# Odd mixer: all sixteen modulation steps behind the second direction's grams in TensorE's order

## The chip, the cores and the metric

The kernel runs on one core of one Trainium2 chip. The metric is the device time of one execution in microseconds (us); the time given for a kernel is the median of its runs. PE is TensorE (matmul), PEld its weight load, DVE VectorE, ACT ScalarE, POOL GpSimd, SP SyncE, whose queue issues nearly all DMAs of this kernel.

## What is computed

Two transformer blocks follow each other on 256 tokens and 256 context tokens of width 1024. The second block has two layers; the change lies in the last one, whose mixer ("odd") joins an RWKV-7 recurrence in both directions and a neighbourhood attention:

```python
mod = jnp.einsum('bd,de->be', jax.nn.silu(c), ada_w[i]) + ada_b[i]
sh1, sc1, g1, sh2, sc2, g2 = jnp.split(mod[:, None, :], 6, -1)
h = rms_norm_2(x, norm1_g[i]) * (1.0 + sc1) + sh1
y, yc = odd_mixer(h, hc, ...)
x = x + g1 * y
h = rms_norm_2(x, norm2_g[i]) * (1.0 + sc2) + sh2
x = x + g2 * expert_choice_ffn(h, moe_router[i], moe_w1[i], moe_w3[i], moe_w2[i])

def wkv7_step(S, inp):                      # one token, one head; the scan runs forward and in reverse
    r, w, k, v, a, b = inp
    sa = jnp.einsum('bhvk,bhk->bhv', S, a)
    S = S * w[:, :, None, :] + sa[..., None] * b[:, :, None, :] + v[..., None] * k[:, :, None, :]
    return S, jnp.einsum('bhvk,bhk->bhv', S, r)
```

The modulation `mod` depends on `c` and on the weights alone. Its last parts (`g1`, `sh2`, `sc2`, `g2`) are first needed where the mixer's result is gated and where the experts are routed, so the kernel is free to compute them at any time before.

## The kernel before

The recurrence is computed in chunks of 64 tokens. For each direction `d` (0, then 1) and each block `b` of two heads (four blocks), `rwkv` runs three parts. `decays(d, b)` multiplies the log decays with a triangular matrix on PE (`py<-tri`), takes exponentials on ACT and forms the products `AR`, `Bh`, `Kh` on DVE and POOL. `within(d, b)` makes the grams `pg<-AR,Bh` on PE and masks them on DVE into `Lx` and `Lc` (L1940). `spill(d, b)` makes the grams `pg<-AR,Kh`, masks them into `MN` (L1953), multiplies them with `V` (`py<-V,MN`), transposes `Bh` and `Kh`, and stores the results to DRAM (`sp`). Between the directions `begin(1)` runs `low_rank` (`py<-low,lwa`, `py<-lwa,low`).

`gather(d)` writes `Lx` and `Lc` to DRAM (L1995) and reads them back in another layout (L1998). `substitute(d)` then inverts 32x32 triangles in 31 steps of two operations on DVE (L2012, L2014), on `fsx` for direction 0 and `sgs` for direction 1, copies the result (L2015) and writes it to DRAM (L2016, L2017). `complete(d)` reads it back (L2031) and runs products on PE (`pg<-fsx,Lx` is its first). Then follow the chunk recurrence and, between its steps, the attention (`natten`: `pS<-nk,nq`, `pt<-cst,p`, `pd<-low,nv`), and after the mixer the sixteen experts, whose weights stream in (L1580).

The modulation is a generator of steps (`mods_steps`, L503). Inside `rwkv` one step loads four tiles `mw` of 128x512 (256 KB each, L550, on SP's queue) and multiplies each with `sil` into another 32 rows of one bank `pd` (`pd<-mw,sil`). Eight steps fill a bank; then come a copy on ACT (`modrow`), four transposes into `pS`, three small operations on DVE, one more transpose (`gatec`) and a small DMA. Two banks are left when `rwkv` begins, so it holds 16 steps: 64 tiles, 64 matmuls (128 records, since a float32 matmul leaves two). The tiles turn in five buffers (tag `n2`, which the attention's `nbias` shares). `fill(n)` takes up to n steps and does nothing when none is left.

Instructions are put in order by a scheduler: each engine's queue is filled by priority, and by readiness as the scheduler's own model has it. The priority is the place in the program, plus `OLATE` = 2000 for what `fill` issues. At run time each engine and SP's queue take their instructions strictly in that order. In the program, `fill` stands behind every block of direction 0 and of direction 1 (`OF` = (2, 2, 2)), so all 16 steps are taken by the end of `within(1, 3)`, and their instructions may go wherever the scheduler finds room.

Of the kernel before, what the change touches and what calls it, by code (L numbers as in the profile page):

```python
# [248 lines left out]
class Kernel:  # L249
# [75 lines left out]

    def mm(self, out, lhsT, rhs, start, stop):
        ins = self.nc.tensor.matmul(out, lhsT, rhs, start=start, stop=stop, skip_group_check=True)  # L327
        if self.pin:
            self.tc.keep_in_program_order(ins)
        return ins  # L330
# [1291 lines left out]

T2 = 16
SUB0, SUB1 = 0, 0
OLATE, OF = 2000, (2, 2, 2)
DECAY = math.exp(-0.5)


# [18 lines left out]
class Odd(Moe):  # L1647
# [201 lines left out]
    def rwkv(self, od, core, m):  # L1849
        nc, tc, a = self.nc, self.tc, self.a  # L1850
# [15 lines left out]
        def begin(d):  # L1866
            S = st[d]

            S["AR"] = core.tile([128, 4, 768], F32, name=f"AR{d}")
            S["ARx"] = S["AR"][:, :, :512].rearrange("p b (i k t) -> p b i k t", k=4, t=64)  # L1870
            S["sp"] = self.dram.tile([4, 128, 3, 512], F32, name=f"sp{d}")
            S["WC"] = core.tile([128, 4, 8], F32, name=f"WC{d}")
            S["gr"] = core.tile([128, 2, 4, 2, 128], F32, name=f"Lx{d}")
            S["sgs"], S["av"] = self.rates[0] if d == 0 else self.low_rank(1, core, "t2", T2, "py")
# [60 lines left out]
        def within(d, b):  # L1935

            for th in range(2):
                p, mask = gram(st[d][b][0], d, b, th)
                L = st[d]["Lc"][:, :, b] if th else st[d]["gr"][:, :, b]
                nc.vector.tensor_tensor(L.rearrange("p t h c -> p h t c"), p, mask, OP.mult)  # L1940
# [44 lines left out]
        def gather(d):  # L1985

            Lx, Lc = st[d]["gr"], st[d]["Lc"]
            scr = [self.dram.tile([4, 32, 32, 32], F32, name=f"scr{d}{i}") for i in range(3)]
            for q in range(4):
                hf, b2 = q // 2, q % 2  # L1990
                ps_ = slice(64 * hf + 32 * b2, 64 * hf + 32 * b2 + 32)
                cs = slice(32 * b2, 32 * b2 + 32)
                for i, gr in ((0, Lx[..., 64 * hf:64 * hf + 64]), (1, Lc)):
                    src = gr[ps_].rearrange("p t b h c -> p (t b h) c")[:, :, cs]
                    nc.sync.dma_start(scr[0][q, 16 * i:16 * i + 16].rearrange("u s t -> s u t"), src)  # L1995
            LM = od.tile([128, 2, 32, 32], F32, name="sgs", bufs=1) if d else st[0]["LX"]
            LM, X = LM[:, 0], LM[:, 1]
            nc.sync.dma_start(LM, scr[0].rearrange("q u s t -> (q u) s t"))  # L1998
            st[d].update(scr=scr, LM=LM, X=X)
# [51 lines left out]
        def fill(n):  # L2051
            with self.later(OLATE, "pS"):
                self.fill(n)
# [3 lines left out]
        for b in range(4):  # L2057
            if b < 3:
                decays(0, b + 1)
            if b == 2:  # L2060
                begin(1)
            within(0, b)
            spill(0, b)
            fill(OF[0])
        gather(0)
        with self.later(SUB0, "pS"):
            substitute(0)
        for b in range(4):
            decays(1, b)
            within(1, b)  # L2070
            fill(OF[1])
        gather(1)
        with self.later(SUB1, "pS"):
            substitute(1)
        for b in range(4):
            spill(1, b)
            fill(OF[2])
        with self.later(OLATE, "pS"):
            self.need(m, 2)

        td = [p.tile([128, 4, 4, 2, 64], F32, name=n, bufs=1) for p, n in ((od, "kk"), (od, "k"))]
# [187 lines left out]
```

## Time and profile before

| | |
|---|---|
| runs | 2823.29, 2827.72, 2834.02 us |
| median | 2827.72 us |
| profiled execution | 2849.02 us, of it span 2847.2 us |
| busy share of the span | PE 91%, DVE 42%, ACT 27%, POOL 11% |
| HBM read | 667.73 MB |

The profiled execution took 0.75% longer than the median; its rows are compared with its own time. The odd mixer's stretch from the first decays to the last chunk is 2041 to 2332 us of the span; the experts' weights fill the rest. In the rows, times are us from the span's start unless marked ns, and a bracket behind a row gives the engine's idle time before it and what ended it. "PEclk" is the granted clock of TensorE, 1.00 for 2.4 GHz and 0.50 for 1.2 GHz.

### The profile page before, as it was taken

What the parts mean: (1) busy time and instruction counts of PE and PEld (TensorE: products, weight loads), DVE (VectorE), ACT (ScalarE), POOL (GpSimd) and SP (SyncE); (2) the same over time, 40 slices, a digit from 0 to 9 for tenths busy, and PEclk for the clock granted to TensorE, in tenths of its full rate; (3) what the DMA queues carried; (4) which work ended last, traced back from release to release, by engine and by line L of the source; (5) the groups of instructions that cost most, each with busy time, mean ns of one, the idle gap of its engine ahead of it and who ended that gap; (6) DMA issues with size and microseconds to landing.
All of it is one profiled execution on the core that took longest, in us unless ns stands there. A gap on an engine that the chain in (4) does not pass through costs nothing.

```text
span 2847.2 us, 34601 instructions
## 1 busy us (share of the span) xinstructions
PE 2597.2 (91%) x13867; PEld 1583.0 (56%) x13867; DVE 1185.8 (42%) x2273; ACT 772.3 (27%) x1394; POOL 302.5 (11%) x370
## 2 busy tenths in 40 slices
PE   7999999997998998989799999989896997888887
PEld 4666788885766896757443333358634784212121
DVE  3355633446456567897411111164539352000000
ACT  3242322222343343376310000044432432000000
POOL 0001400004002004300100000000113130000000
PEclk8999999997999999999899999999986798999999
DMA  7443522223467754244599999942265548999998
GB/s 303 148 163 135 206 104 89 104 89 135 155 210 271 282 182 153 69 152 163 215 420 421 421 421 421 421 164 88 93 194 121 138 154 353 410 421 421 421 422 350
DMA packets 147216, 683.42 MB, mean 240 GB/s; under 512 B 38384, under 2 KB 51568, under 8 KB 71920
## 3 DMA queue, kind: packets, MB, share of 16 engines
q1 hardware_dynamic: 140656, 663.91, 60.9%
q10 hardware_dynamic: 6400, 17.31, 2.0%
q8 instruction: 109, 1.79, 0.3%
q14 instruction: 51, 0.42, 0.0%
HBM read 667.73 MB, written 11.60 MB: 239 GB/s over the span
## 4 chain that ended last, share of the span: by engine, by line
PE 55%; DMA 24%; DVE 7%; issue 2%; ACT 2%; POOL 0%; SPq 0%; ACTq 0%; DVEq 0%; POOLq 0%
DMA w<-in_moe_w 21%; PE pd L327 19%; PE pS L327 12%; PE pu L327 6%; PE pt L327 5%; PE ps L327 3%; PE pg L327 3%; PE pm L327 2%; PE ps L472 1%; DMA w<-in_ada_w 1%; DVE al L364 1%; PE pt L472 1%; DVE fs L2012 1%; PE py L327 1%; DMA w<-in_od_w_in 1%
## 5 line engine op out<-in xcount | busy, mean ns | idle before, releaser
L327 PE MATMUL pu<-w,xs 128*64 128x512 f32 (+1 forms) x2040 | 491.7, 599 | 41.3 <-DMA w<-in_moe_w 41.3
L350 DVE TENSOR_TENSOR wl<-w,wh 128x1024 fp32r<-128x1024 f32 x229 | 283.1, 1239 | 348.6 <-ACT wh L347 348.1
L347 ACT CAST wh<-w 128x1024 fp32r<-128x1024 f32 x250 | 259.5, 1041 | 603.0 <-PE pd L327 260.1
L327 PEld LDWEIGHTS pu<-w,xs 128*64 128x64 f32 (+1 forms) x2040 | 149.7, 123 | 368.8 <-issue 257.4
L327 PE MATMUL pd<-w,hidT 128*64 128x512 f32 (+1 forms) x1024 | 255.4, 598 | 30.5 <-DMA w<-in_moe_w 30.3
L327 PE MATMUL pd<-ah,wh 128*128 128x512 f32 (+2 forms) x656 | 233.6, 361 | 7.8 <-ACT wh L347 3.5
L327 PE MATMUL pd<-al,wh 128*128 128x512 f32 (+2 forms) x656 | 232.1, 355 | 8.7 <-DVE al L364 8.7
L327 PE MATMUL pd<-ah,wl 128*128 128x512 f32 (+1 forms) x648 | 227.5, 352 | 0.0
L1599 ACT ACTIVATE hid<-pu 128x512 f32<-128x512 f32 x24 | 14.2, 597 | 699.4 <-PE pu L327 699.4
L1600 DVE TENSOR_TENSOR hid<-hid,pu 128x512 f32<-128x512 f32 x24 | 16.5, 688 | 425.1 <-PE pu L327 425.1
L327 PEld LDWEIGHTS pd<-w,hidT 128*64 128x64 f32 (+1 forms) x1024 | 74.9, 122 | 201.4 <-issue 117.4
L327 PEld LDWEIGHTS pd<-ah,wh 128*128 128x128 f32 (+1 forms) x656 | 127.8, 196 | 42.8 <-issue 15.8
L327 PEld LDWEIGHTS pd<-al,wh 128*128 128x128 f32 (+1 forms) x656 | 129.0, 197 | 30.2 <-DVE al L364 10.7
L327 PE MATMUL pm<-w,sil 128*32 128x512 f32 x640 | 105.8, 700 | 40.9 <-DMA w<-in_w_mod 24.9
L327 PEld LDWEIGHTS pd<-ah,wl 128*128 128x128 f32 x648 | 127.0, 196 | 22.6 <-issue 8.2
L1609 DVE TENSOR_TENSOR ys<-pd,g 128x512 f32<-128x512 f32 x24 | 16.6, 692 | 288.7 <-PE pd L327 288.7
L1619 DVE TENSOR_TENSOR X<-X,ps 128x512 f32<-128x512 f32 x80 | 54.8, 687 | 113.3 <-PE ps L327 113.3
L1149 DVE SCALAR_TENSOR_TENSOR co<-cv,cols,co 128x512 f32<-128x512 f32 x120 | 100.6, 862 | 0.4
L327 PE MATMUL pS<-al,wh 128*128 128x256 f32 (+1 forms) x264 | 90.7, 345 | 3.7 <-DVE al L364 3.7
L327 PE MATMUL pS<-ah,wh 128*128 128x256 f32 (+1 forms) x264 | 90.0, 342 | 1.4 <-ACT ah L363 1.4
L327 PE MATMUL pS<-ah,wl 128*128 128x256 f32 (+1 forms) x264 | 89.9, 341 | 0.0
L327 PE MATMUL ps<-ys,gt 128*128 128x512 f32 x160 | 82.7, 627 | 2.1 <-DVE X L1619 2.1
(593 smaller groups left out, 4471.7 us busy)
## 6 DMA issues: line engine op xcount, KB each, us to landing
w<-in_moe_w SPq DMA_DIRECT2D x383, 1024.0 KB, 19.8
w<-in_w_mod SPq DMA_DIRECT2D x48, 1024.0 KB, 5.0
w<-in_w_up SPq DMA_DIRECT2D x32, 1024.0 KB, 5.0
w<-in_w_down SPq DMA_DIRECT2D x32, 1024.0 KB, 4.9
w<-in_ada_w SPq DMA_DIRECT2D x32, 1024.0 KB, 5.0
w<-in_w_in SPq DMA_DIRECT2D x20, 1024.0 KB, 4.9
mw<-in_ada_w SPq DMA_DIRECT2D x64, 256.0 KB, 3.7
w<-in_od_w_in SPq DMA_DIRECT2D x13, 1024.0 KB, 4.9
```

What stands on the lines that cost most here:

```text
L327: ins = self.nc.tensor.matmul(out, lhsT, rhs, start=start, stop=stop, skip_group_check=True)
L347: nc.scalar.copy(h, src)
L350: (le or nc.vector).tensor_tensor(l, src, h.bitcast(F32), OP.subtract)
L364: nc.vector.tensor_tensor(l, t, h.bitcast(F32), OP.subtract)
L472: ins = self.nc.tensor.transpose(out, in_, self.ident[:rows, :rows])
L1149: nc.vector.scalar_tensor_tensor(y, CV[:, f, :, t:t + T], self.col(f"dw{t}", f), y, OP.mult, OP.add)
L1599: nc.scalar.activation(hid[:, cs], up["moe_w1_2"][c], AF.Silu)
L1600: nc.vector.tensor_tensor(hid[:, cs], hid[:, cs], up["moe_w3_2"][c], OP.mult)
L1609: nc.vector.tensor_tensor(ys[:, cs], down[c], gate[:, cs], OP.mult)
L1619: nc.vector.tensor_tensor(self.X[tb][:, cs], self.X[tb][:, cs], ps, OP.add)
L2012: nc.vector.tensor_tensor(t, LM[:, s, tr, None].to_broadcast([128, nt_, nj]), X[:, s, None, jr].to_broadcast([128, nt_, nj]), OP.mult)
```

## The change

`fill` no longer stands among the blocks of direction 0 and behind `within(1, b)`. The sixteen steps are taken in the loop over `spill(1, b)`, four behind each block, and every PE instruction of them carries an ordering edge to the last matmul of `within(1, 3)` (`held`), so none may stand ahead of it on PE. The loads of the tiles carry no such edge: they are held by the five buffers and by their place in SP's order.

```diff
     def mm(self, out, lhsT, rhs, start, stop):
         ins = self.nc.tensor.matmul(out, lhsT, rhs, start=start, stop=stop, skip_group_check=True)
+        self.pe = ins
...
-OLATE, OF = 2000, (2, 2, 2)
+OLATE = 2000
...
             within(0, b)
             spill(0, b)
-            fill(OF[0])
         gather(0)
         with self.later(SUB0, "pS"):
             substitute(0)
         for b in range(4):
             decays(1, b)
             within(1, b)
-            fill(OF[1])
+        held = self.pe
         gather(1)
         with self.later(SUB1, "pS"):
             substitute(1)
         for b in range(4):
             spill(1, b)
-            fill(OF[2])
-        with self.later(OLATE, "pS"):
+            with tc.issue_after(held.ins):
+                fill(4)
+        with self.later(OLATE, "pS"), tc.issue_after(held.ins):
             self.need(m, 2)
```

In the changed kernel line numbers behind 327 are one higher. A row of the order is a run of equal instructions of one engine; `32x512` is one tile's matmul.

PE in direction 0, before, from the last transpose of block 0 to the first gram of block 2:

```order
L472 MATMUL py<-cst,Kh 128x128 x4
L327 MATMUL pg<-AR_13923,Kh 64x128 x2
L327 MATMUL pd<-mw,sil 32x512 x2
L327 MATMUL py<-tri,sgs 128x256
L327 MATMUL py<-tri,mix 128x256
L327 MATMUL py<-tri,sgs 128x256
L327 MATMUL py<-tri,mix 128x256
L327 MATMUL pd<-mw,sil 32x512
L327 MATMUL pg<-AR_13923,Kh 64x64 x8
L327 MATMUL pd<-mw,sil 32x512
```

The same place now:

```order
L473 MATMUL py<-cst,Kh 128x128 x4
L327 MATMUL pg<-AR_13923,Kh 64x128 x3
L327 MATMUL py<-tri,sgs 128x256
L327 MATMUL py<-tri,mix 128x256
L327 MATMUL py<-tri,sgs 128x256
L327 MATMUL py<-tri,mix 128x256
L327 MATMUL pg<-AR_13923,Kh 64x128 x2
L327 MATMUL pg<-AR_13923,Kh 64x64 x8
```

The blocks of direction 0 and 1 follow each other without `pd<-mw,sil`; all 64 of these stand further back.

PE ahead of `complete(0)`, before, from the last product of `spill(1, 3)`:

```order
L327 MATMUL py<-V,MN 64x64 x24
L472 MATMUL py<-cst,Bh 128x128 x4
L472 MATMUL py<-cst,Kh 128x128 x4
L327 MATMUL pg<-fsx,Lx_13926 64x32 x32
```

The same place now:

```order
L327 MATMUL py<-V,MN 64x64 x8
L473 MATMUL py<-cst,Bh 128x128 x4
L327 MATMUL pd<-mw,sil 32x512 x3
L473 MATMUL py<-cst,Kh 128x128 x4
L327 MATMUL pd<-mw,sil 32x512 x8
L473 MATMUL pS<-cst,modrow 128x128 x4
L327 MATMUL pd<-mw,sil 32x512 x3
L473 MATMUL pS<-cst,gatec 16x128
L327 MATMUL pd<-mw,sil 32x512 x29
L473 MATMUL pS<-cst,modrow 128x128 x4
L473 MATMUL pS<-cst,gatec 16x128
L327 MATMUL pg<-fsx,Lx_13926 64x32 x32
```

Of the 64 matmuls, 21 stand ahead of these rows, between the parts of `spill(1, b)`; the other 43 and both banks' transposes stand in them, ahead of the first product of `complete(0)`.

SP's queue where the result of `substitute(1)` goes out and comes back, before:

```order
L2016 DMA scr_15024<-sgs 128x1024
L2017 DMA scr_15025<-sgs 128x1024
L2031 DMA k<-scr_15025 32x32x32 x4
L2031 DMA sgs<-scr_15024 32x32x32 x4
L1835 DMA nbias<-in_na_bias 128x512 x3
L2134 DMA mv<-sp_13924 128x512
```

The same place now:

```order
L551 DMA mw<-in_ada_w 128x512 x2
L2017 DMA scr_14798<-sgs 128x1024
L2018 DMA scr_14799<-sgs 128x1024
L1984 DMA sp_14242<-zt 64x4x128 x4
L551 DMA mw<-in_ada_w 128x512 x3
L2032 DMA k<-scr_14799 32x32x32 x4
L2032 DMA sgs<-scr_14798 32x32x32 x4
L551 DMA mw<-in_ada_w 128x512 x33
L1836 DMA nbias<-in_na_bias 128x512 x4
L2135 DMA mv<-sp_13924 128x512
```

Of the 64 loads, 28 stand ahead of `substitute(1)`'s result (5 ahead of the first block, 6 behind the gather of direction 1, 17 between the two substitutions' results), 3 between its way out and its way back, and 33 behind both; before, all 64 stood ahead of direction 1's gather.

## Rows read from the trace of the kernel before

**Rows 1.** Busy us by engine in stretches of the odd mixer.

```profile
core 0: us, PE busy (x) PEld busy (x) DVE busy (x) ACT busy (x) POOL busy (x), PEclk, DMA share, GB/s
2041.00:2084.00 43.00, 37.83 (x398) 17.54 (x398) 19.46 (x32) 16.38 (x48) 16.05 (x17) 0.94 0.73 219
2084.00:2107.00 23.00, 23.00 (x40) 5.21 (x43) 7.31 (x14) 8.18 (x13) 0.00 (x0) 0.50 0.32 95
2119.00:2176.00 57.00, 41.05 (x417) 22.10 (x417) 47.95 (x108) 19.60 (x54) 24.78 (x23) 0.76 0.53 145
2176.00:2204.00 28.00, 16.96 (x258) 14.53 (x256) 26.21 (x73) 5.76 (x12) 3.85 (x3) 0.62 0.65 147
2202.00:2246.00 44.00, 44.00 (x559) 31.57 (x559) 16.83 (x39) 15.68 (x31) 1.80 (x1) 0.50 0.51 127
2246.00:2332.00 86.00, 86.00 (x974) 72.01 (x973) 44.00 (x92) 36.24 (x72) 25.36 (x34) 0.99 0.44 131
```

**Rows 2.** Chain that ended last, 2041 to 2119 us, shares by line.

```profile
by line: PE pd L327 36.5%; PE py L327 28.7%; DMA mw<-in_ada_w 19.4%; PE pg L327 8.8%; DMA fsx<-scr 8.3%; PE py L472 3.0%; PE pS L472 1.7%; ACT tri L1863 0.7%; SPq L550 0.4%; issue 0.4%; SPq L1998 0.1%
```

**Rows 3.** PE in order of time, direction 0 and low_rank: start, us.

```profile
2062.54 0.39 PE L327 MATMUL py<-tri,sgs 128*128 128x256 f32 x1
...
2070.60 0.67 PE L327 MATMUL pg<-AR,Bh 64*64 64x128 f32 x16
...
2072.78 0.66 PE L472 MATMUL py<-cst,Bh 128*128 128x128 f32 x4
...
2084.36 3.78 PE L327 MATMUL py<-low,lwa 64*128 64x512 f32 x4
...
2089.91 2.07 PE L327 MATMUL py<-low,lwa 64*128 64x512 f32 x2
...
2108.71 1.12 PE L327 MATMUL py<-lwa,low 64*128 64x512 f32 x2
```

**Rows 4.** DVE in order of time: grams masked, substitutions' first and last steps.

```profile
2049.51 0.68 DVE L1940 TENSOR_TENSOR Lx<-pg,cst 128x512 f32<-128x512 f32 x1
...
2113.30 0.42 DVE L1940 TENSOR_TENSOR Lc<-pg,cst 128x256 f32<-128x256 f32 x1 [4.74 <-PE pg L327]
...
2124.90 0.19 DVE L2012 TENSOR_TENSOR fs<-fsx 128x31 f32<-128x31 f32 x1 [7.27 <-DMA fsx<-scr]
...
2203.85 0.19 DVE L2014 TENSOR_TENSOR sgs<-sgs,fs 128x31 f32<-128x31 f32 x1
```

**Rows 5.** From issue to landing, the gathers' two read-backs (L1998).

```profile
DMA to landing us min/median/max: 3.4/5.0/6.5
```

**Rows 6.** SP's queue in order of time, with us that the run took.

```profile
2065.22 7.38 SPq L550 DMA_DIRECT2D mw<-in_ada_w  x8
...
2131.91 10.67 SPq L550 DMA_DIRECT2D mw<-in_ada_w  x9
...
2211.81 4.24 SPq L2031 DMA_DIRECT2D sgs<-scr  x4
...
2332.06 29.42 SPq L1580 DMA_DIRECT2D w<-in_moe_w  x15
```

**Rows 7.** From issue to landing, the 64 tiles mw.

```profile
DMA to landing us min/median/max: 2.6/3.7/5.9
```

**Rows 8.** PE in order of time, modulations' ends and complete's first product.

```profile
2088.07 1.91 PE L327 MATMUL pd<-mw,sil 128*32 128x512 f32 x2
...
2201.99 3.63 PE L327 MATMUL pg<-fsx,Lx 64*64 64x32 f32 x64
```

**Rows 9.** ACT behind a full bank of the modulation: start, us.

```profile
2090.02 0.59 ACT L523 COPY modrow<-pd 128x512 f32<-128x512 f32 x1 [0.83 <-PE pd L327]
```

**Rows 10.** Chain pieces of PE with the same shape at either clock: start, us, what.

```profile
2205.62 3.71 PE pS L327 x4
...
2251.75 1.91 PE pS L327 x4
```

**Rows 11.** PE at the span's beginning, where it runs modulations alone: busy, PEclk.

```profile
24.00:32.00 8.00, 4.40 (x20) 0.50 1.01 419
```

## The prediction

> **What bounds the kernel now.** I read the busy times by stretch first [rows 1], then the chain of waits, then single engines in order of time. From 2041 to 2107 us PE is busy 60.8 of 66 us, and DVE 26.8; from 2119 to 2204 it is the other way round, DVE 74.2 of 85 and PE 58.0. So the first part of the mixer waits for PE, the two substitutions wait for DVE, and from 2202 to 2332 PE is busy without a gap (44 of 44, 86 of 86) [rows 1]. The chain of the first part shows what PE does there: of 78 us 36.5% are modulation matmuls, 19.4% loads of their tiles and 0.4% their issue, together 43.9 us [rows 2]. The experts' first loads go out when the mixer ends, at 2332.06 [rows 6], so a shift of the mixer's end is a shift of the kernel's end.
>
> **What is taken away: the modulations among direction 0.** At most the whole 43.9 us goes. But the chain then shows the next-late work, and I walk through it in three pieces, each at 2.4 and at 1.2 GHz, since which clock PE is granted with this work alone no row shows.
>
> First piece, to the third block's first triangular product at 2062.54 [rows 3]. The first gram is masked at 2049.51, straight behind other DVE work, without a wait [rows 4]: nothing is won up to there. What is left on PE then are nine groups of grams, products with V and transposes, of which a gram takes 0.67 us and a block's transposes 0.66 at 2.4 GHz [rows 3]: I estimate 5.5 us for the nine, and 10 at 1.2 GHz. So the product comes at 2055.5 to 2060: 2.5 to 7 us won.
>
> Second piece, from there to `low_rank` at 2084.36 [rows 3], 21.8 us before. One block's nine groups pass, 5.5 us as before, with some 3 in which PE waits for ACT's exponentials and DVE's products, and then the last block's decays, 1.7: I estimate 10 us at 2.4 GHz and 14 at 1.2, where PE's own time covers the wait: 8 to 12 won.
>
> Third piece, `low_rank` to the last gram masked at 2113.30 [rows 3, 4], 28.9 us before. Eight products of 2.07 us at 1.2 GHz are 16.6 us, of 1.12 at 2.4 GHz 9.0 [rows 3]; there the chain through DVE and ACT is longer, some 14. With 1 us for the gram: 11 to 14 won. In sum 22 to 33 us; I take 28.
>
> The gather's read-back landed after 6.5 us among the tiles' loads and after 3.4 without [rows 5]. It has none beside it now; I take 2 us won, with 0 and 3 as ends.
>
> **What stays: the substitutions.** From 2124.90 to 2203.85 DVE inverts both triangles, 79 us [rows 4], nearly always busy [rows 1]. The modulations weigh little there: six small operations. The order of DVE puts two `MN` more of direction 0 inside (shapes that take 0.68 and 0.42 us as `Lx` and `Lc` [rows 4]), and the first decays of direction 1 are ready later against the substitution's start. I charge 3 us, with 1 and 5 as ends. `substitute(1)` so ends 28 + 2 - 3 = 27 us earlier, at 2177 instead of 2204.
>
> **What is added: the modulations behind.** Here the order of SP decides. Of 64 loads 31 can be out when `substitute(1)`'s result has been written; the other 33 stand behind its read-back, and PE has all of them ahead of `complete(0)`'s first product. Queued behind that on PE are all of the completion, the attention and the recurrence; none of it can pass. Counted from the last step of `substitute(1)`:
>
> - the read-back's last issue ends at 2211.81 + 4.24 = 2216.05, 12.2 us behind 2203.85 [rows 4, 6]: 12 us. The waits in it (copy, write, memset, read) stay;
> - five tiles go out at once, 2 us; the other 28 follow as buffers come free. Free of other work the ring made eight tiles in 7.38 us and nine in 10.67, 0.92 to 1.19 us each [rows 6]. At 1.2 GHz a group takes 1.91 us [rows 8], at 2.4 half of it, which the ring of five carries; I take 1.15, near the slower row, so 32.2 us;
> - the last lands after 3.7 us [rows 7] and is multiplied in 1.9 [rows 8];
> - the second bank's end: the copy takes 0.59 us [rows 9], then come four transposes (0.66 for such a group [rows 3], 1.1 at 1.2 GHz), three small operations on DVE and the last transpose, each behind the one before: I estimate 3.4 us.
>
> That is 12 + 2 + 32.2 + 3.7 + 1.9 + 3.4 = 55.2 us. Before, `complete(0)` began at 2201.99 [rows 8], 1.9 us ahead of that last step, since it needs direction 0 alone. So the move costs 57 us on the path and gives back 27: **30 us later**. Its ends: a ring at 0.92, PE at 2.4 GHz and a gain of 35 leave 12 + 2 + 25.8 + 3.7 + 1 + 3 + 1.9 - 35 = 14; a ring at 1.19 and a gain of 17 (22 + 0 - 5) give 58.2 - 17 = 41.
>
> Behind it nothing hides the delay: PE has no gap until 2332 [rows 1]. The attention's `nbias`, now behind the 33 loads too, lands while `complete(0)`'s first product runs (3.63 us [rows 8]); without that cover it would cost the 3.7 us of a landing [rows 7].
>
> **TensorE's clock.** From 2202 to 2246 PE is granted 0.50 all the time [rows 1], so that the same work could take less: four products of the attention take 3.71 us there and 1.91 at 2.4 GHz [rows 10]. By these shapes I estimate 17 us between the two clocks. I leave the 17 us out of the sum: modulations alone, 4.40 us busy of 8, were granted 0.50 at the span's beginning [rows 11], and between 2084 and 2107, with `low_rank` and no gap at all, 0.50 too [rows 1].
> The Trainium skill, page "TensorE: Matmul & The Clock Gate", section "Part 1: The HAM clock gate", says the opposite of such a stream: the throttled state is the default, and sustained activity releases it. By that rule the 33 tiles would bring the clock up ahead of `complete(0)`; by the rows of these two stretches they would not. By rule the sum would be smaller by those 17 us and by the faster ring; it is the first rival.
>
> **The rivals.**
> *The clock comes up and stays up* (not slower). With no modulation between them the decays run at 2.4 GHz, so that 33 + 3 - 1 = 35 us are won; the ring runs at 0.92 and PE at its fast groups, 49.4 us; and completion and attention win 17. That is 49.4 - 35 - 17 = -3, or 2846 in the profile and 2825 as a median. For it: PE was granted 0.94 on average from 2041 to 2084 [rows 1]. Against it: rows 11, the 23 us from 2084, and that the modulations were half of what kept PE busy there. It decides at `complete(0)`: if PE is granted 1.00 there, most of the loss is gone.
> *PE holds DVE up* (slower still). `spill(1, b)`'s grams now stand behind tiles whose loads SP may issue only behind `substitute(0)`'s result. If two of DVE's `MN` wait for such a tile in the middle of `substitute(1)`, each wait is a landing and a group, 3.7 + 1.9 us [rows 7, 8], and `substitute(1)` ends 11 us later: +41, 2869 as a median. For it: DVE keeps its order, and the grams of blocks 2 and 3 stand behind the 13th and the 14th tile. Against it: DVE has ten to fifteen steps to do before it asks for them.
> *The ring fills its gaps better than I think*, so that most of the 33 are in by the read-back: the order of SP forbids it.
>
> **How the numbers follow.** The sum is made against the profiled execution: 2849.0 + 30 = 2879. That execution took 0.75% longer than the median of 2827.7, and I carry the difference over: 2827.7 + 30 = 2858. A measurement of this kernel can tell about 0.5% from no change, 14 us: faster is below 2814, slower above 2842. Forecast 65%, nearly all of it slower; PE holding DVE up 12%, all slower; the clock 23%, of which about 16 within 14 us and 7 faster, since its ends reach 12 us below its value. Together faster 7%, same 17%, slower 76%. The range takes the forecast's ends of +14 and +41 and goes down into the clock's case, to +4 and up to +45: 2832 to 2873; it leaves out most of the clock's case and a part of the second rival, some 2 in 10.
>
> **What would show it.** In the profile after: the last gram of direction 0 masked between 2080 and 2091; the read-back of `gather(0)` landing in 3.4 to 5 us; the last step of `substitute(1)` near 2177 (2171 to 2187); then DVE and ACT idle while SP issues 33 tiles at 0.9 to 1.2 us each; `pg<-fsx,Lx` near 2232; and the experts' first load near 2362. Before those 33, PE idle for some microseconds, waiting for tiles. It would be wrong if `complete(0)` began before 2216, if PE were granted 1.00 there, or if the substitutions no longer took about 79 us.

## The result and the profile after

The changed kernel took 2866.41 us as a median (2859.64 to 2876.03), the kernel before 2830.68 in the same series: a ratio of 1.0133 with an interval of 1.0107 to 1.0159, so 30 to 45 us slower. A second series gave 1.0137 (1.0096 to 1.0179). The forecast was 2858 with a range of 2832 to 2873.

The profiled execution of the changed kernel took 2862.35 us, only 13 us more than that of before (2849.02). That the profiles stand 13 us apart and the medians 36 is the question of this study, and most of the answer is the clock.

The stretches of the mixer first, as in [rows 1] (the first number behind the stretch is its length, then busy us of PE, PEld, DVE, ACT and POOL, PEclk, DMA share, GB/s):

```profile
2042.00:2069.00 27.00, 19.84 (x309) 16.27 (x309) 16.69 (x28) 13.05 (x39) 12.76 (x14) 0.71 0.16 38
2069.00:2083.00 14.00, 11.72 (x47) 4.53 (x48) 9.32 (x15) 9.53 (x20) 3.78 (x5) 0.71 0.23 62
2097.00:2181.00 84.00, 51.56 (x607) 31.83 (x608) 74.89 (x176) 22.54 (x61) 27.01 (x24) 0.71 0.55 144
2181.00:2205.00 24.00, 12.47 (x30) 2.55 (x28) 0.78 (x1) 1.17 (x2) 1.80 (x1) 0.70 1.03 248
2205.00:2232.00 27.00, 22.95 (x59) 3.63 (x57) 0.45 (x3) 0.25 (x1) 0.00 (x0) 0.95 0.76 251
2238.54:2347.41 108.87, 108.81 (x1531) 89.32 (x1531) 58.44 (x121) 50.93 (x104) 25.63 (x34) 1.00 0.41 127
```

The row from 2205 to 2232 is new: DVE, ACT and POOL do nothing (0.45, 0.25 and 0 us of 27), and the kernel waits for tiles of the modulation. DVE in order of time, the rows that answer to [rows 4]:

```profile
2088.44 0.42 DVE L1941 TENSOR_TENSOR Lc<-pg,cst 128x256 f32<-128x256 f32 x1 [3.65 <-PE pg L327]
2097.17 0.19 DVE L2013 TENSOR_TENSOR fs<-fsx 128x31 f32<-128x31 f32 x1 [7.98 <-DMA fsx<-scr]
...
2180.49 0.19 DVE L2015 TENSOR_TENSOR sgs<-sgs,fs 128x31 f32<-128x31 f32 x1
```

SP's queue from the end of the second substitution, against [rows 6]: result out, three tiles, the read-back, then 33 tiles in one row of 33.98 us; the attention's `nbias` and the experts follow.

```profile
2182.88 0.42 SPq L2017 DMA_DIRECT2D scr<-sgs  x1
2183.35 0.42 SPq L2018 DMA_DIRECT2D scr<-sgs  x1
2183.87 4.23 SPq L1984 DMA_DIRECT2D sp<-zt  x4
2188.20 1.52 SPq L551 DMA_DIRECT2D mw<-in_ada_w  x3
2189.78 4.01 SPq L2032 DMA_DIRECT2D k<-scr  x4
2193.89 3.64 SPq L2032 DMA_DIRECT2D sgs<-scr  x4
2197.63 33.98 SPq L551 DMA_DIRECT2D mw<-in_ada_w  x33
2232.03 23.75 SPq L1836 DMA_DIRECT2D nbias<-in_na_bias  x4
...
2347.41 28.67 SPq L1581 DMA_DIRECT2D w<-in_moe_w  x15
```

PE at the same place, the rows that answer to [rows 8]:

```profile
2234.66 1.68 PE L327 MATMUL pd<-mw,sil 128*32 128x512 f32 x4 [0.76 <-DMA mw<-in_ada_w]
2237.02 0.66 PE L473 MATMUL pS<-cst,modrow 128*128 128x128 f32 x4 [0.68 <-ACT modrow L524]
2238.34 0.27 PE L473 MATMUL pS<-cst,gatec 128*16 128x128 f32 x1 [0.67 <-DVE gatec L537]
2238.54 2.06 PE L327 MATMUL pg<-fsx,Lx 64*64 64x32 f32 x64
```

`complete(0)` begins at 2238.54, 58.05 us behind the last step of `substitute(1)`; before, it was 1.86 us ahead of that step [rows 4, 8]. PE's waits in the tail ended with a tile, 16.8 us in eleven waits from 2181 to 2238; only at the ends of the two banks did it wait for ACT's copy (twice 0.7 us) and DVE's `gatec` (0.67).

### The profile page after: what moved, and what is told of

Read it like the earlier page. It is cut to its first block, busy times and chain, and to the rows that moved or that the text cites. A ratio compares the mean times of both kernels' runs of the same rounds, so it can differ in the third digit from the quotient of the medians.

```text
span 2860.5 us, 34616 instructions
## 1 busy us (share of the span) xinstructions
PE 2581.0 (90%) x13867; PEld 1573.6 (55%) x13867; DVE 1186.8 (41%) x2273; ACT 770.7 (27%) x1394; POOL 302.7 (11%) x370
## 4 chain that ended last, share of the span: by engine, by line
PE 55%; DMA 23%; DVE 7%; issue 2%; ACT 2%; SPq 1%; POOL 0%; ACTq 0%; DVEq 0%; POOLq 0%
DMA w<-in_moe_w 19%; PE pd L327 19%; PE pS L327 12%; PE pu L327 8%; PE pt L327 5%; PE ps L327 3%; PE pg L327 2%; PE pm L327 2%; DMA mw<-in_ada_w 1%; DVE al L365 1%; DMA w<-in_ada_w 1%; PE ps L473 1%; PE pt L473 1%; PE pO L327 1%; DVE co L1150 1%
## 5 line engine op out<-in xcount | busy, mean ns | idle before, releaser
L1620 DVE TENSOR_TENSOR X<-X,ps 128x512 f32<-128x512 f32 x80 | 54.8, 687 | 113.3 <-PE ps L327 113.3
```

The costliest lines, as they stand in the source:

```text
L1620: nc.vector.tensor_tensor(self.X[tb][:, cs], self.X[tb][:, cs], ps, OP.add)
```

## The experiments

Eleven runs were made, four of them of the two kernels without an edit, in three groups. A group shares its runs of the kernel before, so times of different groups are best compared by their ratio to it. Positions in the mixer are counted from the first `py<-tri` of direction 0, since what lies ahead of it varies by some us from execution to execution.

**The kernel before and the changed kernel, again.** No edit. Two theories on the 13 against 36 us.

> The kernel before, once more, to see a second profiled execution of the same program. In the two profiles the change cost 13 us (2849.0 to 2862.4), in the medians 36 (2830.7 to 2866.4). Theory A, the clock differs from execution to execution: this profile shows TensorE's clock at 1.00 between the first product of complete(0) and the end of the attention's first part (44 us before), that stretch takes about 22 us, and the profiled execution takes about 2828 instead of 2849. Theory B, the clock hangs on what stands ahead in PE's order (substitution with gaps: 0.50; a stream of modulations: 1.00): the profile shows 0.50 again, complete(0) to the first expert load takes 130 us again, and the execution takes about 2849, while the timed ones stay near 2830; then the 21 us between profiled and timed executions lie elsewhere.

> The changed kernel, once more. Both theories: complete(0) begins about 37 us later than in the profile of before, counted from the first tile's load; 33 loads behind the read-back take 34 us. Theory A (clock by execution): complete(0) to the first expert load may take 109 us (clock 1.00) or 130 (0.50), and the profiled time is 2862 or about 2883. Theory B (clock by what stands ahead): 109 us again. Timed: ratio 1.010 to 1.016.

> The kernel before, a third profiled execution, for the clock alone. In the first two TensorE was granted 0.50 through low_rank and 0.50 for 44 us of the completion (2849.0 us), and 1.00 through low_rank and 0.50 for some 12 us of the completion (about 2822 us). If the clock differs by execution in each of the two places by itself, a third mixture may appear, and the mixer takes between 272 and 291 us from its first decays to the first expert load; if the first profile was the exception, it takes about 272 again.

> The changed kernel, a third profiled execution, for the clock. In the first two complete(0) began 196 and 199 us behind the first decays, and the way from there to the first expert load took 109 us (clock 1.00 throughout) and 120 (0.50 for some 25 us). Again 196 to 199, and 109 to 131 by the clock that this execution is granted.

Measured: the two further profiled executions of before took 2822.07 and 2822.93 us, those of the changed kernel 2877.96 and 2877.53. The six executions (us; from the rows of the first triangular product, of the substitutions' first and last step, of `complete(0)`'s first product and of the experts' first load):

| execution | `substitute(0)` begins | `substitute(1)` ends | `complete(0)` begins | from there to the experts' first load | whole |
|---|---|---|---|---|---|
| before, as shown ahead | 83.8 | 162.7 | 160.9 | 130.1 | 2849.0 |
| before2 | 73.2 | 152.2 | 150.3 | 121.9 | 2822.1 |
| before3 | 68.4 | 147.8 | 146.0 | 121.8 | 2822.9 |
| after | 54.9 | 138.3 | 196.3 | 108.9 | 2862.4 |
| after2 | 54.9 | 140.5 | 198.8 | 120.4 | 2878.0 |
| after3 | 55.5 | 138.0 | 197.0 | 121.1 | 2877.5 |

Two stretches of the same program differ. One is `low_rank`, from the view by stretch of before2 (the stretch that had 0.50 in [rows 1]) and from PE in order of time (the first product, which took 3.78 us in [rows 3]):

```profile
2077.00:2100.00 23.00, 22.22 (x125) 6.54 (x129) 8.86 (x17) 9.98 (x17) 2.03 (x3) 1.00 0.73 210
```

```profile
2078.36 1.98 PE L327 MATMUL py<-low,lwa 64*128 64x512 f32 x4
```

The other is the beginning of the completion. In before2 and before3 it began at 0.50 too (the first product took 3.63 us), but stayed there for some 26 us instead of 44. Before3:

```profile
2185.09:2210.00 24.91, 24.91 (x342) 18.84 (x342) 10.21 (x25) 8.77 (x17) 1.80 (x1) 0.50 0.61 134
```

In after2 PE had no gap in the first of these stretches, the second is the whole way:

```profile
2253.00:2266.00 13.00, 13.00 (x157) 9.60 (x154) 3.71 (x8) 4.70 (x9) 0.00 (x0) 0.50 0.08 21
2241.54:2361.95 120.41, 119.60 (x1531) 96.83 (x1531) 58.53 (x121) 51.41 (x104) 25.64 (x34) 0.90 0.39 115
```

So the core of theory A holds: which clock is granted there, and for how long, differs from execution to execution of one program. Its expectation for before2, 1.00 from `complete(0)` on, was not met. The first profile of before was the exception, the slowest of all executions of that kernel (the timed ones lie between 2820 and 2837 us), with 0.50 through both stretches; that of the changed kernel was one of its fastest. The means of the three come near the difference of the medians: `complete(0)` begins at 197.4 instead of 152.4, 45.0 us later; the way from there is 116.8 instead of 124.6, 7.8 us shorter; together 37.2 us, beside 36 to 40 measured. The whole executions differ by 41.3 us in the mean, 4 of them outside the mixer. One execution on either side makes nearly all of the 7.8: without before and after, `complete(0)` begins 49.7 us later and the way is 120.8 instead of 121.9. So this is a split of six executions, and that the change itself shortens the way is not shown.

**Nearly no modulation in the new place (few).**

```diff
             for k in range(KT):
+                if self.modpool and k < KT - 1:
+                    yield
+                    continue
```

> The changed kernel with one of every eight modulation steps: 8 tiles instead of 64 (the other seven steps of each bank are left out, so the last parts of the modulation are wrong). What is measured is the whole price of the 56 tiles in their new place. If the tail behind the read-back is what complete(0) waits for, it begins within 3 us of the last step of substitute(1) (about 55 us earlier than in the changed kernel) while that last step stays within 3 us of the changed kernel's. Theory A (clock by execution): the time falls by about 57 us against the changed kernel, to about 2809, and the completion can have either clock. Theory B (the stream of modulations brings the clock up): without the stream the completion runs at 0.50, 21 us of the 57 are lost again, and the time is about 2830.

Measured: 2818.70 us, a ratio of 0.9948 (0.9926 to 0.9970) to before. The last step of `substitute(1)` came at 135.0, `complete(0)` at 141.7, behind the last products of `spill(1, 3)`. So the 56 tiles cost 51 us in their new place (2869.6 - 2818.7, the same series), and only 11 in the old one (2830.0 - 2818.7). By this run a better place could win some 11 us; that is an estimate and no strict bound, since 8 tiles still run. Two expectations were missed: `complete(0)` came 6.7 us behind the last step, not within 3, and the time lies between the 2809 and the 2830 of the two theories. The completion took 124.5 us at a mean clock of 0.90, as in two of three executions of either kernel, though nothing of the stream was left; its first product took 2.06 us, at 1.00. So the clock can be up there without the stream.

**Is it the loads or PE (oneload, short)?**

```diff
-            ws = [self.modpool() for _ in range(4)]
-            for g, wt in enumerate(ws):
-                self.nc.sync.dma_start(wt, src[:, g * 512:(g + 1) * 512])
-            return ws
+            wt = self.modpool()
+            self.nc.sync.dma_start(wt, src[:, :512])
+            return [wt] * 4
```

> The changed kernel with 16 loads instead of 64: of the four tiles of a step only the first is loaded, and all four matmuls read it (so the last parts of the modulation are wrong). PE's work and its order's edge stay. Theory L (the loads, held up behind the read-back and by the five buffers, set the tail): the tail falls from 58 us between the last step of substitute(1) and complete(0) to about 12 + 2 + 8 loads of 1.03 + 3.7 + 1.9 + 3.4, some 31 us or less, and the time by about 27 us, to about 2842. Theory P (PE's 33 groups of 1.04 us at 2.4 GHz, 1.91 at 1.2, set it): the tail stays at 45 us or more and the time above 2855. Since PE's groups and the loads have nearly the same pace in the trace (1.03 us a load), a result between the two is possible if each hides half of the other; then the wait for the first tiles behind the read-back, 12 us, is what falls away.

```diff
+                    n = 64 if self.modpool and 0 < k < KT - 1 else 512
-                    self.mm(ps[32 * g:32 * g + 32, :], sl[:, k, :], ws[g] if self.modpool else ws[:, g * 512:(g + 1) * 512],
-                            k == 0, k == KT - 1)
+                    self.mm(ps[32 * g:32 * g + 32, :n], sl[:, k, :],
+                            ws[g][:, :n] if self.modpool else ws[:, g * 512:(g + 1) * 512], k == 0, k == KT - 1)
```

> The changed kernel with all 64 loads, but six of every eight steps multiply only the first 64 of a tile's 512 columns (so the last parts of the modulation are wrong). The loads and both orders stay nearly as they are (31 loads behind the read-back instead of 33). Theory L (loads set the tail): complete(0) still begins 50 us or more behind the last step of substitute(1), and the time stays within 8 us of the changed kernel's 2866 to 2870. Theory P (PE sets it): the tail falls below 35 us and the time below 2848. On the clock: if the stream of modulations is what brings TensorE's clock up for complete(0), this kernel starts it at 0.50.

Measured: with a quarter of the loads and all of PE's matmuls 2824.38 us (0.9991, 0.9975 to 1.0006), the time of before; with all loads and a fraction of PE's work 2863.14 (1.0145, 1.0120 to 1.0170), that of the changed kernel. PE in oneload: the last four steps (32 records) run in one row under the substitution, and `complete(0)` starts 4.7 us behind its end (2176.74), not 58:

```profile
2165.87 3.64 PE L327 MATMUL pd<-mw,sil 128*32 128x512 f32 x32
...
2181.45 3.63 PE L327 MATMUL pg<-fsx,Lx 64*64 64x32 f32 x64
```

The first row shows that oneload changed a second thing. Its 16 matmuls took 3.64 us, 0.23 each, where one by itself (two records) takes 1.04; earlier in the same run four took 1.07:

```profile
2143.34 1.04 PE L327 MATMUL pd<-mw,sil 128*32 128x512 f32 x2
2144.88 1.07 PE L327 MATMUL pd<-mw,sil 128*32 128x512 f32 x8 [0.50 <-DMA mw<-in_ada_w]
```

The four matmuls of a step write separate 32 rows of the bank, and when no tile is awaited between them they overlap. So oneload took time from PE too, and does not part loads from PE by itself; short does.

And SP's queue in short, whose `complete(0)` begins at 2231.48, 53.6 us behind the last step (2177.91):

```profile
2196.16 28.32 SPq L552 DMA_DIRECT2D mw<-in_ada_w  x31
```

Theory L holds: in short, where most tiles need an eighth of the multiplication, a tile still took 0.91 us (28.32 for 31) instead of 1.03, and the tail was only 4.5 us shorter. Oneload fell by more than expected, about 40 us, not 27, since tiles that don't have to be fetched leave PE free to do all 64 groups under the substitutions, and four at a time. There DVE is the bound (74.1 of 85.5 us busy in oneload), and the groups cost little: `substitute(1)` ended at 140.5 in oneload, and at 135.0 in few.

The clock in short went against its expectation (0.50 at `complete(0)` if the stream is what brings it up): it was low in the tail and at 1.00 from `complete(0)` to the experts' first load.

```profile
2205.00:2231.48 26.48, 14.27 (x57) 5.10 (x57) 0.65 (x5) 0.59 (x1) 0.00 (x0) 0.55 0.78 258
2231.48:2342.66 111.18, 109.26 (x1531) 89.55 (x1531) 57.59 (x121) 50.97 (x104) 25.34 (x34) 1.00 0.42 125
```

With few, and with after2, where the clock fell behind the stream, the stream of tiles is neither needed for 1.00 there nor enough.

**All steps behind direction 0 (behind0).** The edge goes to the last matmul of direction 0, and the steps are taken among direction 1's decays and grams.

```diff
             spill(0, b)
+        held = self.pe
         gather(0)
...
             within(1, b)
-        held = self.pe
+            with tc.issue_after(held.ins):
+                fill(4)
```

> All sixteen steps behind direction 0 as in the change, but taken among the blocks of direction 1's decays and grams, with the edge to the last matmul of direction 0's spill; all 64 loads then stand ahead of the read-back of substitute(1) in SP's order, and 17 of the 64 matmuls in one row ahead of complete(0). If the 33 loads behind the read-back are the main price of the change: direction 0 stays as fast as in the changed kernel (last gram masked about 46 us behind the first decays), and complete(0) begins 10 to 20 us behind the last step of substitute(1) instead of 57; the time is 2815 to 2828. If instead PE's own work is the price, wherever it stands behind direction 0: the two substitutions stretch from 85 to 100 us or more, because DVE waits for grams behind tiles, and the time is 2835 or more.

Measured: 2831.58 us (1.0013, 0.9993 to 1.0034), the time of before, between the two expectations. Direction 0 is as fast as in the changed kernel (`substitute(0)` begins at 54.8). But the grams of direction 1 now stand behind tiles, so that `gather(1)` is late and DVE waits between the substitutions:

```profile
2156.46 0.19 DVE L2013 TENSOR_TENSOR fs<-sgs 128x31 f32<-128x31 f32 x1 [7.74 <-DMA sgs<-scr]
```

The two substitutions take 90.2 us instead of 79, and `complete(0)` begins 16.4 us behind the last step. Each theory has a part: with the loads ahead of the read-back the tail is 42 us shorter, and PE's order, with tiles ahead of the grams, costs 11, of which the wait shown is 7.7.

**The read-back on another queue (queue).**

```diff
-                    nc.sync.dma_start(dst[ps_, :, cs], sc[q].rearrange("u s t -> s u t"))
+                    (nc.scalar if d else nc.sync).dma_start(dst[ps_, :, cs], sc[q].rearrange("u s t -> s u t"))
```

> The changed kernel with the eight DMAs of direction 1's read-back issued on ACT's queue instead of SP's. The tiles then no longer stand behind the read-back, only behind the write of the result; 36 of the 64 loads stand there. If the read-back ahead of them costs the 12 + 2 us that the prediction charged (16 us from the last step of substitute(1) to the first of the 33 loads, by the trace of the changed kernel), the first of the late loads goes out some 13 us earlier and three more loads are late: the tail falls from 58 to about 48 us and the time by about 10, to 2855 to 2860. If the ring of five alone paces the tail, whatever stands in the queue, the tail stays within 4 us of 58 and the time within 5 of 2867.

Measured: 2874.25 us (1.0151, 1.0108 to 1.0193), no gain; the tail is 56.6 us. The first late load goes out 7.3 us behind the last step instead of 17.1, yet the row of loads takes 42.25 us for 36 tiles, 1.17 each, instead of 33.98 for 33, 1.03 each:

```profile
2188.51 42.25 SPq L551 DMA_DIRECT2D mw<-in_ada_w  x36
```

The read-back now stands on ACT's queue ahead of the copy that ends the first bank, and PE with its ring of tiles stands behind that copy. ACT in order of time, the idle time in the bracket, and PE's own wait:

```profile
2201.26 0.59 ACT L524 COPY modrow<-pd 128x512 f32<-128x512 f32 x1 [15.12 <-DMA sgs<-scr]
```

```profile
2201.90 1.11 PE L473 MATMUL pS<-cst,modrow 128*128 128x128 f32 x4 [3.68 <-ACT modrow L524]
```

This run doesn't settle what the place behind the read-back costs by itself: the hindrance was moved to another queue, not taken away.

**Half of each tile (half).**

```diff
+                    n = 256 if self.modpool and 0 < k < KT - 1 else 512
-                self.nc.sync.dma_start(wt, src[:, g * 512:(g + 1) * 512])
+                self.nc.sync.dma_start(wt[:, :n], src[:, g * 512:g * 512 + n])
```

> The changed kernel with 64 loads, of which 48 bring and multiply only the first 256 of a tile's 512 columns (128 KB; so the last parts of the modulation are wrong). It measures what paces the ring of five behind the read-back, 1.03 us a tile. If it is the way of one load (issue, landing, multiplication, next issue in the same buffer, some 5 us shared by five buffers), the pace falls only by the shorter multiplication and transfer, to 0.75 to 0.9 us, and the tail by 5 to 8 us. If it is the rate at which bytes come in (256 KB in 1.03 us is 254 GB/s), the pace halves, to 0.5 to 0.6 us, and the tail falls by 11 to 14 us.

Measured: 2848.84 us (1.0079, 1.0056 to 1.0102), some 15 us less than the changed kernel by the ratios (1.0133 and 1.0137); the tail is 45.4 us (2177.35 to 2222.73), 12.7 less. PE in the tail, ten records for five tiles:

```profile
2207.81 2.63 PE L327 MATMUL pd<-mw,sil 128*32 128x256 f32 x10 [0.28 <-DMA mw<-in_ada_w]
2210.66 2.64 PE L327 MATMUL pd<-mw,sil 128*32 128x256 f32 x10 [0.22 <-DMA mw<-in_ada_w]
```

Five tiles turn in 2.85 us, 0.57 us each, so the pace nearly halves: the second expectation. The issues' view shows how: the time from issue to landing, first in the changed kernel's tail, then in half's.

```profile
DMA to landing us min/median/max: 2.7/3.8/5.0
```

```profile
DMA to landing us min/median/max: 2.0/2.2/3.6
```

A buffer's round is landing, multiplication and the next issue: 5 x 1.03 = 5.15 us is 3.8 + 1.04 and 0.3; 5 x 0.57 = 2.85 is 2.2 + 0.6 and little else. The round is shared by five buffers as in the first expectation, but the landing itself goes with the bytes, which that expectation had left out. PE was busy 2.63 of the 2.85 us, so in half the multiplications alone would have set nearly the same pace; that they don't in the changed kernel is short's result.

**A kernel between the two (split).** The first bank among direction 0, the second behind its last matmul:

```diff
             spill(0, b)
+            held = self.pe
+            fill(2)
...
             within(1, b)
+            with tc.issue_after(held.ins):
+                fill(2)
```

> A kernel between the two: the first bank's eight steps among direction 0's blocks (two behind each), the second bank's eight behind direction 0's last matmul, among direction 1's decays and grams; all loads go out ahead of substitute(0)'s result and no tile is multiplied behind direction 1's first spill. With 56 of 64 tiles left out the time was 2818.7 against 2830.0, so no place of the modulations can win much more than 11 us against the kernel before. If direction 0's price of the modulations goes by their number there (18 to 28 us for about 50 tiles), 32 tiles cost it 11 to 18 us; the second bank lies in the substitution, where PE idles, and stretches it by 3 to 6 us: 2823 to 2830. If the eight steps cost direction 0 as much as the sixteen did, or the substitutions stretch by 11 us as with all sixteen there, it is 2832 or more.

Measured: 2821.29 us (0.9988, 0.9975 to 1.0002): not to be told from before, and just below the 2823 to 2830 expected. By the medians it is 4 us below before in its group, where few, which runs an eighth of the tiles, was 11 below. `substitute(0)` begins at 60.1, `substitute(1)` ends at 145.5, `complete(0)` starts at 144.8, without a tail. It is some 40 us faster than the changed kernel by the ratios; as a gain against before it isn't clear.

## Why the prediction came out right, and where it was off

**What is taken away.** Step by step this was right against the profile it was made from. From the first triangular product the third block's came at 18.0 (2060.19) instead of 21.4, 3.5 us won (2.5 to 7 foreseen); `low_rank` at 28.7 (2070.89) instead of 43.2, the second piece 11.1 (8 to 12); the last gram masked at 46.2 instead of 72.2, the third piece 11.4 (11 to 14). The read-back landed after 3.8 us, 2.7 won (2). `substitute(0)` began 28.8 us earlier: the 30 of the forecast. The substitutions took 83.3 instead of 79.0 us, 4.4 more (3; on its cause see the second rival). So the last step of `substitute(1)` came 24.5 us earlier (27).

**The failed step** is the one that carried the difference over: "That execution took 0.75% longer than the median of 2827.7, and I carry the difference over". Those 21 us were no scale on the whole span: of the 26 us between that execution and before3, 23 lay in the mixer (290.9 against 267.8 us from the first triangular product to the experts' first load), where [rows 1] show 0.50, and one of these stretches is the one that the change shortens. With three executions on either side `substitute(0)` begins 20.0 us earlier (75.1 to 55.1), not 28.8, and the last step 15.3 (154.3 to 138.9), not 27. The gain was over-sized by 12 us.

In the terms of the sum it is the third piece that didn't hold beyond that profile. From `low_rank` to the last gram masked it took 28.9 us there, but 18.4 in before2 and 19.3 in before3; the changed kernel took 17.5, 17.5 and 17.6. So against these two 1 to 2 us were won, not 11 to 14. And the changed kernel's `low_rank` fell to 0.50 in all three executions, PE in after:

```profile
2070.89 1.12 PE L327 MATMUL py<-low,lwa 64*128 64x512 f32 x2
...
2079.19 3.78 PE L327 MATMUL py<-lwa,low 64*128 64x512 f32 x4 [0.22 <-DVE sg L1818]
```

**What is added.** 58.05 and the 1.86 before it, 59.9 us, where 57 was foreseen. The terms: to the first late load 17.1 us (12: the stores of `zt` and three more tiles stand between, 4.23 + 1.52 us, in part under the wait for the write to land; the order of SP had shown them and the sum left them out); the row of 33 tiles 33.98 (2 + 32.2, at 1.03 us a tile); landing, multiplication and the bank's end 6.9 (9.0, since PE was at 2.4 GHz). That 33 loads stand behind the read-back and that this, not PE's 33 groups, makes the price, short shows, and oneload fits it.

**Behind the tail.** "Nothing hides the delay" was right, PE has no gap there; that the clock stays at 0.50 from there to the attention, as the sum had it, held for none of the three executions throughout (0.50 for some 25 us in two). The way to the experts' first load was 7.8 us shorter on average, not 0. So the sum was 30 = 57 - 27, and the runs show 37 = 60 - 15 - 8: a gain over-sized by 12, a tail under-sized by 3, and a share of 8 behind the tail that was left out and makes up for half of that. That these errors have opposite signs, and that the 8 hang on one execution on either side, is luck, and part of why the forecast came so near.

**The first rival, the clock,** came true in one execution of three: PE was granted 1.00 from `complete(0)` on, and the way was 108.9 us, in an execution of 2862 us, far from the rival's 2825. Its other half did not: without the modulations PE was granted 0.71 between 2042 and 2083, less than with the modulations between them (0.94 [rows 1]). In the stream of tiles the trace agrees with the rule of the Trainium skill that was set against the forecast ("TensorE: Matmul & The Clock Gate", "Part 1: The HAM clock gate", sustained activity releases the throttle): 0.95 from 2205 to 2232. But in after2 and after3 the clock fell back to 0.50 in the completion, for PE without a gap, so that the price drawn from the rule was no safe one.

**The second rival,** PE holding DVE up, came at a third of its price. DVE did not wait for an `MN`, but for the sum that takes in PE's products with `V`, and these stood behind a tile. DVE in order of time, and PE's wait ahead of it:

```profile
2150.37 0.42 DVE L1972 TENSOR_TENSOR nkv<-nkv,py 128x256 f32<-128x256 f32 x1 [3.87 <-ACT MV L1967]
```

```profile
2146.05 1.91 PE L327 MATMUL pd<-mw,sil 128*32 128x512 f32 x2 [5.65 <-DMA mw<-in_ada_w]
2147.89 1.86 PE L327 MATMUL py<-V,MN 64*64 64x64 f32 x29
```

In before DVE had no such wait between the substitutions' first and last step, and its work is the same on both sides (74.2 us in 79.2, 74.6 in 83.6). So the 3 us that the forecast charged for the substitutions had nearly the right size and the wrong cause: it is this wait, 3.87 us and a short one, 4.3 together (6.7 in after2, 3.8 in after3), not two more `MN` or later decays. In behind0, where the grams themselves stand behind tiles, the same mechanism cost 11 us.

**The marks.** The last gram masked at 2088.44 (2080 to 2091), the last step at 2180.49 (2171 to 2187), the loads at 1.03 us (0.9 to 1.2), DVE and ACT idle: as foreseen. `complete(0)` at 2238.54 (near 2232) and the experts' first load at 2347.41, 2361.95 and 2361.34 (near 2362): the two at the usual clock hit the last mark, but by two errors that cancel: `complete(0)` 8 to 10 us late, and a way some 10 us shorter than the 130.1 that the forecast went by. Two signs of being wrong appeared: PE was granted 1.00 at `complete(0)` in after, and the substitutions took 83.3 us, not about 79.

## What to carry to other kernels

Work that has no place on an engine's critical stretch has one under a wait only if its data can be there too: the matmuls were nearly free under DVE's substitutions where no tile was awaited (oneload), but in the changed kernel the loads, held by five buffers and by a queue in strict order, came out behind the next thing that everybody waits for. Ask of a step that is moved back which loads can be issued ahead of the last thing on their queue, and price the rest by the ring's round. And take more than one profiled execution before a stretch is costed: where a stretch shows 0.50 with PE fully busy, the next execution may show 1.00, and a gain read from it is worth less in the median.

## What the runs showed of the hardware

- The granted clock in a stretch of full PE work differs between executions of one program: `low_rank` ran at 0.50 in one execution of before and at 1.00 in two, the way from `complete(0)` on took 109, 120 and 121 us in the changed kernel and 130, 122 and 122 in the kernel before.
- The clock can fall with PE busy without a gap: after2 had its first product of `complete(0)` in 2.80 us, then 0.50 from 2253 to 2266. In short it was 0.55 ahead of `complete(0)` and 1.00 from there on.
- Four matmuls into separate 32 rows of one bank overlap: 16 of them took 3.64 us in oneload, where one by itself took 1.04.
- A 256 KB tile landed after 3.8 us with five in flight, a 128 KB tile after 2.2; the stream came at 251 GB/s, while the experts' weights come at some 410 to 420 in the kernel before.
